# The first norm's sums and row factors: from matrix-engine transposes to x with tokens on partitions and 32x32 squares on VectorE

## The chip, the cores and the metric

The kernel runs on one core of one Trainium2 chip. The metric is the device time of one execution in microseconds (us), the median of several runs; less is better. The core has a matrix engine (PE, whose weight loads the profile lists apart as PEld), VectorE (DVE), ScalarE (ACT), GpSimd (POOL) and a queue engine (SP) that issues most of the transfers.

## What is computed

One layer of a hybrid encoder on 512 tokens of width 1024, in float32. What matters here is its beginning:

```python
def rms_norm(x, g):
    y = xf * lax.rsqrt(jnp.mean(xf * xf, axis=-1, keepdims=True) + EPS)
    return (y * g.astype(jnp.float32)).astype(x.dtype)
...
h = rms_norm(x, attn_norm_g[l])
proj = h @ w_in[l]
xr, gate, q, k, v = jnp.split(proj, [...], axis=-1)
xr = centred_depthwise_conv(xr, conv_w[l], conv_b[l])
h_f = rg_lru(xr, ...)
```

Then come the recurrent gates and scans, dilated attention, an output projection and an MLP, each with norms of its own. The factor of the first norm, one number for each token, is `rsqrt(mean(x*x) + EPS)`.

## The kernel before, in words

**Products.** The first operand of the projection is x turned, features on the 128 partitions and the 512 tokens along the row, eight tiles `k`. It is multiplied by the gain `g` but not by the token's factor; that factor is applied to the results. Each float32 operand is split into a high and a low part and each product is three matmuls (`mm3`: high by high, high by low, low by high; lines L312, L313, L314). A chunk of weights is 128x1024 numbers (512 KB) in a tile `wraw`; its high part `whi` is written by `conv_hi` (on ACT, L247, or for chunks 4, 7, 8, 9 on DVE, L245) and its low part `wlo` by `conv_lo` (DVE, L269). After the low part is made, `emit_dma` issues the load of a later chunk on SP.

**The first tiles.** `cvx(k)` makes the high and low parts of x tile k and of the first three weight columns that come with it (tiles `tw` and `wraw`, loaded at L341). PE accumulates four blocks of results, `pxr[0]` to `pxr[3]`: the first three during the pass over k (L453, then `mm3`), the fourth afterwards with chunk 3 of the weights (`xmm`). After them it goes on with chunk 4 (tile `pp`, the gate's first block).

**The first norm before.** After each `cvx(k)`, `sq(k)` squares the x tile on ACT (L372) and `addsq` adds the squares on DVE (L375), until one 128x512 tile `sqx` holds sums over the eight tiles; what is left is the sum over the 128 partitions. PE turns that tile in four 128x128 transposes (`turned`, tile `pcs`, L430), set between two blocks of the last k; DVE adds up the rows (L435) and adds EPS (L414); POOL raises to the power -0.5 (L417, 128x4 numbers, `rcol`: tokens on partitions). For the results, which have tokens along the row, a tile is needed that holds the 512 factors in every partition: PE makes it with four more transposes from a broadcast of `rcol` (`prow`, L409) and ACT copies it to `rrow`, called `rstd` in the code (L423).

**What hangs on rstd.** `conv_a(t)` multiplies block t by `rstd` (DVE, L496) and starts the convolution on ACT (L498); `conv_b(t)` does the other three taps on DVE (L503 to L505). `lru_gates` then multiplies the four results `xc` by the gates' weights on PE (tile `pg`, L528), t = 0 to 3 in order, and ACT evacuates (L532). In PE's order this stands behind the eight steps of chunk 4 and ahead of chunk 5.

**What sets the order.** Each engine executes its instructions in the order in which the code is written, and waits for the others by semaphores. The order of PE, ACT, DVE and POOL is the program's; before the change that of SP's queue was a scheduler's.

Of the kernel before, what the change touches and what calls it, by code (L numbers as in the profile page):

```python
# [12 lines left out]
FT = mybir.dt.float32  # L13
# [85 lines left out]
def hybrid_kernel(ctx: ExitStack, tc, xw0, xw, xn, w_in, w_v, w_out, w_up, w_dn, gates, vecs, bias, fg, out):  # L99
# [13 lines left out]
    def g_(name, dt=FT, shape=(P, S)):  # L113
        return work.tile(list(shape), dt, name=name, tag="g", bufs=NG)
# [19 lines left out]
    make_identity(nc, ident)  # L134
    mhalf = consts.tile([P, 4], FT, name="mhalf")
    nc.gpsimd.memset(mhalf, -0.5)
# [191 lines left out]
    xwt, w3 = [], []  # L328
    for k in range(KD):
        if 4 <= k < 7:  # L330
            xwt.append(stream.tile([P, 1024], FT, name="wraw", tag="wraw", bufs=3)[:, :XW])
        else:
            xwt.append(work.tile([P, 1024], FT, name="tw", tag="tw", bufs=4)[:, :XW if k else XG + 3 * P])
        if k == 0:
            nc.sync.dma_start(xwt[0][:, :XG], xw0[:, :XG])
            nc.sync.dma_start(xwt[0][:, XG:], xw0[:, XG:])
            nc.gpsimd.tensor_copy(ag, xwt[0][:, S:XG])
            w03 = g_("w03")[:, :P]
            nc.sync.dma_start(w03, w_in[3][:, :P])
        else:  # L340
            nc.sync.dma_start(xwt[k], xw[k - 1])  # L341
        if k == 6:
            nc.sync.dma_start(vt, vecs)

    sqx = {}

    def cvx(k):
        x, w = xwt[k][:, :S], xwt[k][:, S if k else XG:]
        g = ag[:, k:k + 1] if k else xwt[0][:, S:S + 1]
        hi, lo = g_("w3h", FR), g_("w3l", FR)  # L350
        if k < 2:
            c = (2 * P, 3 * P)[k]
            act(h_hi[:, k, :c], x[:, :c], AF.Copy, scale=g)
            nc.vector.tensor_scalar(h_hi[:, k, c:], x[:, c:], g, None, op0=OP.mult)
            if k == 0:
                nc.vector.tensor_copy(hi[:, :2 * P], w[:, :2 * P])
                act(hi[:, 2 * P:3 * P], w[:, 2 * P:], AF.Copy)
            else:
                nc.vector.tensor_copy(hi[:, :3 * P], w)
        else:  # L360
            act(h_hi[:, k, :], x, AF.Copy, scale=g)
            act(hi[:, :3 * P], w, AF.Copy)
        stt(h_lo[:, k, :], x, g, f(h_hi)[:, k, :], op0=OP.mult, op1=OP.subtract)
        nc.vector.tensor_tensor(lo[:, :3 * P], w, f(hi)[:, :3 * P], op=OP.subtract)
        if k == 0:
            act(hi[:, 3 * P:], w03, AF.Copy)
            nc.vector.tensor_tensor(lo[:, 3 * P:], w03, f(hi)[:, 3 * P:], op=OP.subtract)
        w3.append((hi, lo))

    def sq(k):  # L370
        sqx[k] = g_("sqx")
        act(sqx[k], xwt[k][:, :S], AF.Square)  # L372

    def addsq(k):
        nc.vector.tensor_tensor(sqx[0], sqx[0], sqx.pop(k), op=OP.add)  # L375

    cvx(0)
    sq(0)
    for k in range(1, KD):
        cvx(k)  # L380
        if 5 <= k < 7:
            next(spc)
        sq(k)
        if k >= 2:
            addsq(k - 1)
    emit_dma()
    for t in range(4):
        gate_load(t)
    emit_dma()
    addsq(7)  # L390
    emit_dma()

# [12 lines left out]

    def rows_of(cols, tag):
        pr = ps_("prow", tag)
        for tt in range(4):
            nc.tensor.transpose(pr[:, tt * P:(tt + 1) * P], cols(tt), ident)  # L409
        return pr  # L410

    def rstd_cols(ssc, n):
        v = small("rv", 4)
        nc.vector.tensor_scalar(v, ssc, 1.0 / n, EPS, op0=OP.mult, op1=OP.add)  # L414
        r = consts.tile([P, 4], FT, name="rcol_%d" % st["rc"])
        st["rc"] += 1
        nc.gpsimd.tensor_tensor(r, v, mhalf, op=OP.pow)  # L417
        return r

    def row_tile(cols, tag):  # L420
        pr = rows_of(lambda tt: fan(cols, tt, 1, P), tag)
        r = g_("rrow")
        act(r, pr, AF.Copy)  # L423
        return r


    def turned(ss, tag):
        pc = ps_("pcs", tag)
        for tt in range(4):
            nc.tensor.transpose(pc[:, tt * P:(tt + 1) * P], ss[:, tt * P:(tt + 1) * P], ident)  # L430
        return pc

    def row_sums(pc):
        c = small("cs", 4)
        nc.vector.tensor_reduce(c, pc.rearrange("p (t c) -> p t c", t=4), axis=mybir.AxisListType.X, op=OP.add)  # L435
        return c

# [11 lines left out]
    for k in range(KD):  # L449
# [1386 lines left out]
```

## Time and profile before

| what | value |
|---|---|
| median of 3 runs (lowest to highest) | 523.14 us (522.76 to 523.55) |
| the profiled execution, its own time | 522.93 us |
| its span, first to last instruction | 521.1 us |
| PE busy | 514.8 us (99%) |
| DVE busy | 430.5 us (83%) |
| ACT busy | 352.3 us (68%) |
| POOL busy | 66.2 us (13%) |
| mean granted clock of PE | 0.999 |

The span is 1.8 us less than the execution's own time, and that execution lies 0.2 us below the median. Times of the trace count from the start of the span. A row of the timeline gives start, duration, engine, line, what is written and what is read, and in brackets the idle time of the engine ahead of it with what ended it. Matmuls are pipelined: the duration of one is longer than the distance from its start to the next one's, so that distance is read for what a matmul costs.

### The profile page before, as it was taken

How to read it: one execution, taken by the hardware profiler on the slowest of the kernel's cores; microseconds unless marked ns; L12 is line 12 of the kernel's file. 1: busy time of each engine (PE TensorE's matmuls, PEld its weight loads, DVE VectorE, ACT ScalarE, POOL GpSimd, SP SyncE). 2: the span in 40 equal slices, each digit the busy share in tenths (PEclk: the TensorE clock that was granted, in tenths of full speed). 3: DMA queues.
4: the chain of work that ended last, by engine and by line, in shares of the span. 5: the costliest groups of instructions: out<-in, count | busy, mean ns of one | idle time of the engine just before them, and what ended most of it. 6: DMA issues, size and time to landing. Idle time of an engine off the chain costs nothing.

```text
span 521.1 us, 8223 instructions
## 1 busy us (share of the span) xinstructions
PE 514.8 (99%) x3021; PEld 444.0 (85%) x3021; DVE 430.5 (83%) x667; ACT 352.3 (68%) x571; POOL 66.2 (13%) x89
## 2 busy tenths in 40 slices
PE   9999999999999999999999999999999999999995
PEld 7857888887778788899999888889999999888884
DVE  6998985887789998898789987789766978986885
ACT  7579946777759757685568655675667577655655
POOL 0183000000010410000300412001100300231000
PEclk9999999999999999999999999999999999999999
DMA  8736555477376799847695899967986496799704
GB/s 289 224 92 198 160 155 181 117 203 209 82 250 234 196 206 285 309 148 170 154 209 158 212 275 276 309 259 165 302 259 164 117 229 211 154 290 257 198 1 162
DMA packets 40329, 105.15 MB, mean 202 GB/s; under 512 B 5056, under 2 KB 13376, under 8 KB 40288
## 3 DMA queue, kind: packets, MB, share of 16 engines
q1 hardware_dynamic: 32448, 78.07, 44.9%
q0 software_dynamic: 7696, 26.32, 27.3%
q8 instruction: 24, 0.39, 0.3%
q10 hardware_dynamic: 144, 0.23, 0.1%
q14 instruction: 17, 0.14, 0.1%
HBM read 95.59 MB, written 4.29 MB: 192 GB/s over the span
## 4 chain that ended last, share of the span: by engine, by line
PE 99%; ACT 0%; DVE 0%; issue 0%
PE pu L312 10%; PE pu L314 10%; PE pu L313 10%; PE pd L314 10%; PE pd L312 10%; PE pd L313 10%; PE pqk L312 3%; PE pqk L314 3%; PE pqk L313 3%; PE pwo L312 3%; PE pwo L314 3%; PE pwo L313 3%; PE pav L941 2%; PE pt L841 2%; PE ps L805 2%; PE pp L312 1%
## 5 line engine op out<-in xcount | busy, mean ns | idle before, releaser
L269 DVE TENSOR_TENSOR wlo<-wraw,whi 128x1024 fp32r<-128x1024 f32 x71 | 86.5, 1219 | 22.2 <-ACT whi L247 22.0
L247 ACT ACTIVATE whi<-wraw 128x1024 fp32r<-128x1024 f32 x67 | 70.8, 1058 | 36.8 <-PE pd L314 19.0
L313 PE MATMUL pd<-wlo,ah 128*128 128x512 f32 (+1 forms) x195 | 75.2, 386 | 0.0
L312 PE MATMUL pd<-whi,ah 128*128 128x512 f32 (+1 forms) x195 | 75.2, 386 | 0.0
L314 PE MATMUL pd<-whi,al 128*128 128x512 f32 (+1 forms) x195 | 75.2, 386 | 0.0
L313 PE MATMUL pu<-hl,whi 128*128 128x256 f32 x224 | 63.4, 283 | 0.0
L314 PE MATMUL pu<-hh,wlo 128*128 128x256 f32 x224 | 63.4, 283 | 0.0
L312 PE MATMUL pu<-hh,whi 128*128 128x256 f32 x224 | 63.4, 283 | 0.0
L312 PE MATMUL pu<-h2h,whi 128*128 128x256 f32 (+1 forms) x200 | 60.1, 301 | 0.0
L313 PE MATMUL pu<-h2l,whi 128*128 128x256 f32 (+1 forms) x200 | 60.0, 300 | 0.0
L314 PE MATMUL pu<-h2h,wlo 128*128 128x256 f32 (+1 forms) x200 | 60.0, 300 | 0.0
L269 DVE TENSOR_TENSOR wlo<-tw,whi 128x1024 fp32r<-128x1024 f32 x37 | 45.2, 1222 | 17.6 <-ACT whi L247 17.6
L247 ACT ACTIVATE whi<-tw 128x1024 fp32r<-128x1024 f32 x38 | 40.1, 1058 | 24.9 <-PE pd L314 6.3
L312 PEld LDWEIGHTS pu<-hh,whi 128*128 128x128 f32 x224 | 43.0, 192 | 0.0
L313 PEld LDWEIGHTS pu<-hl,whi 128*128 128x128 f32 x224 | 43.0, 192 | 0.0
L314 PEld LDWEIGHTS pu<-hh,wlo 128*128 128x128 f32 x224 | 43.0, 192 | 0.0
L247 ACT ACTIVATE whi<-ts 128x1024 fp32r<-128x1024 f32 x24 | 25.5, 1061 | 25.9 <-PE pd L314 18.4
L313 PEld LDWEIGHTS pd<-wlo,ah 128*128 128x128 f32 x195 | 36.6, 188 | 7.4
L314 PEld LDWEIGHTS pd<-whi,al 128*128 128x128 f32 x195 | 36.6, 188 | 7.4
L312 PEld LDWEIGHTS pd<-whi,ah 128*128 128x128 f32 x195 | 36.6, 188 | 7.3
L314 PEld LDWEIGHTS pu<-h2h,wlo 128*128 128x128 f32 x200 | 38.3, 191 | 1.3
L313 PEld LDWEIGHTS pu<-h2l,whi 128*128 128x128 f32 x200 | 38.3, 191 | 1.3
(283 smaller groups left out, 1221.4 us busy)
## 6 DMA issues: line engine op xcount, KB each, us to landing
wraw<-in_w_up_dram SPq DMA_DIRECT2D x25, 512.0 KB, 4.0
ts<-in_w_dn_dram POOLq DMA_DIRECT2D x24, 512.0 KB, 12.9
wraw<-in_w_dn_dram SPq DMA_DIRECT2D x24, 512.0 KB, 10.4
tw<-in_w_up_dram SPq DMA_DIRECT2D x15, 512.0 KB, 5.3
tw<-in_w_up_dram POOLq DMA_DIRECT2D x15, 512.0 KB, 7.5
wraw<-in_w_in_dram SPq DMA_DIRECT2D x13, 512.0 KB, 3.5
ts<-in_w_dn_dram SPq DMA_DIRECT2D x8, 512.0 KB, 8.6
tw<-in_w_dn_dram SPq DMA_DIRECT2D x8, 512.0 KB, 6.8
```

What stands on the lines that cost most here:

```text
L247: act(hi, raws[i], AF.Copy)
L269: nc.vector.tensor_tensor(lo, r, f(splits[i][0]), op=OP.subtract)
L312: nc.tensor.matmul(o, lhsT=a[0], rhs=b[0], start=bool(first), stop=False, skip_group_check=on)
L313: nc.tensor.matmul(o, lhsT=a[0], rhs=b[1], start=False, stop=False, skip_group_check=on)
L314: nc.tensor.matmul(o, lhsT=a[1], rhs=b[0], start=False, stop=bool(last), skip_group_check=on)
L805: nc.tensor.matmul(pss[e][:, :NK], lhsT=qs_[p, a][r, P * qt:P * qt + P], rhs=kks[p][r, b, w:w + NK], start=i == 0, stop=i == 2)
L841: nc.tensor.transpose(pt[:, i * P:(i + 1) * P], en[h][qt][:, k:k + P], ident)
L941: nc.tensor.matmul(pav[p][a, co], lhsT=vs[:, jt, h * DH:(h + 1) * DH], rhs=et[h, jt][:, ci], start=jt == 0 and i == 0, stop=jt == 3 and i ...
```

## The change

The sums of squares are taken from a second copy of x that has tokens on partitions. `xn` is an input that the kernel had already (it is read much later for the residual); eight blocks of it, 128x512 numbers (256 KB) each, are now also loaded at the beginning as `xs`, two for each 128 tokens. A block's row sum is one instruction: on ACT a square with an accumulator for blocks 0, 1, 2, 4 and 6, on DVE a multiply with an accumulator (`tensor_tensor_reduce`) for 3, 5 and 7. They give `ss8`, 128x8 numbers. Sixteen DVE instructions of 32x4 numbers each add the two halves and EPS and copy each group of 32 partitions into all four groups (`rv16`, 128x16). POOL's power runs on those 128x16 numbers (`r16`). ACT writes each of the 16 columns 32 times (`rfan`, 128x512), and one DVE transpose of 32x32 squares makes `rstd` of it. `rcol` is copied out of `r16` by four small POOL instructions. The eight PE transposes, the ACT squares and the DVE adds of before are gone.

Other things move with it. SP's queue in this part is now in written order, with the eight loads `xs` ahead of chunk 3, and chunk 3 is loaded as two halves. Chunk 3 is converted after the sixteen small instructions: DVE makes the high and the low part of its first half and the low part of its second, ACT the high part of the second. Chunk 4 is converted after the transpose. ACT's conversion of chunk 5 comes after `conv_a(1)`.

```diff
+        def sq(i):
+            c = ss8[:, 4 * (i % 2) + i // 2:4 * (i % 2) + i // 2 + 1]
+            if i in (3, 5, 7):
+                nc.vector.tensor_tensor_reduce(xs[i], xs[i], xs[i], 1.0 / D, 0.0, OP.mult, OP.add, c)
+            else:
+                act(xs[i], xs[i], AF.Square, scale=D ** -0.5, accum_out=c)
...
-    def sq(k):
-        sqx[k] = g_("sqx")
-        act(sqx[k], xwt[k][:, :S], AF.Square)
-
-    def addsq(k):
-        nc.vector.tensor_tensor(sqx[0], sqx[0], sqx.pop(k), op=OP.add)
...
+        for i in range(8):
+            load_xs(i)
+        plain.popleft()
+        raws[3] = stream.tile([P, 1024], FT, name="wraw", tag="wraw", bufs=3)
+        for c in (slice(0, S), slice(S, 2 * S)):
+            nc.sync.dma_start(raws[3][:, c], w_in[3][:, c])
...
-            if k == KD - 1 and t == 0:
-                sqt = turned(sqx[0], "et")
...
-    conv_hi(3)
-    conv_lo(3)
-    rcol = rstd_cols(row_sums(sqt), D)
+    for i in range(8):
+        sq(i)
+    rv16 = small("rv16", 16)
+    for a in range(4):
+        r = slice(32 * a, 32 * a + 32)
+        for b in range(4):
+            stt(by_group(rv16)[32 * b:32 * b + 32, a], ss8[r, :4], EPS, ss8[r, 4:], op0=OP.add, op1=OP.add)
+    r16 = consts.tile([P, 16], FT, name="r16")
+    nc.gpsimd.tensor_tensor(r16, rv16, mhalf, op=OP.pow)
+    hi, lo = [stream.tile([P, 1024], FR, name=n, tag=n, bufs=4) for n in ("whi", "wlo")]
+    r = raws.pop(3)
+    splits[3] = (hi, lo)
+    c = slice(0, S)
+    nc.vector.tensor_copy(hi[:, c], r[:, c])
+    nc.vector.tensor_tensor(lo[:, c], r[:, c], f(hi)[:, c], op=OP.subtract)
+    c = slice(S, 2 * S)
+    act(hi[:, c], r[:, c], AF.Copy)
+    nc.vector.tensor_tensor(lo[:, c], r[:, c], f(hi)[:, c], op=OP.subtract)
+    emit_dma()
+    rfan, rstd = g_("rfan"), g_("rrow")
+    act(rfan.rearrange("p (b i) -> p b i", i=32), fan(r16, 0, 16, 32), AF.Copy)
+    nc.vector.transpose(rstd, rfan)
     conv_hi(4)
-    conv_hi(5)
     nc.gpsimd.dma_start(bt, bias)
     conv_lo(4)
-    xmm(range(1, 3))
-    rstd = row_tile(rcol, "et")
+    xmm(range(1, 2))
     conv_a(0, pxr[0])
     conv_a(1, pxr[1])
+    conv_hi(5)
     next(spc)
     cneg, chalf = next(spc)
+    rcol = consts.tile([P, 4], FT, name="rcol")
+    for a in range(4):
+        r = slice(32 * a, 32 * a + 32)
+        nc.gpsimd.tensor_copy(rcol[r], by_group(r16)[r, a])
     conv_b(0)
     act(warm, epsb, AF.Sigmoid)
-    xmm(range(3, KD))
+    xmm(range(2, KD))
```

On PE, at the last k of the first pass and at the beginning of chunk 3, the difference reads as follows (`whi` and `wlo` are the parts of chunk 3 here):

```order
 L313 MATMUL pxr<-h_lo,w3h 128x512
 L314 MATMUL pxr<-h_hi,w3l 128x512
-L430 MATMUL pcs<-ident,sqx 128x128 x4
 L312 MATMUL pxr<-h_hi,w3h 128x512
 L313 MATMUL pxr<-h_lo,w3h 128x512
```

The four transposes go; the second four, L409, go in the same way from between the second and the third step of chunk 3, and nothing else moves on PE.

On DVE, from the end of `cvx(7)` to the first use of `rstd`, the order before was this (`sqx` the squares, `wraw` to `wlo` at L269 first chunk 3 and then chunk 4):

```order
L364 TENSOR_TENSOR w3l<-tw,w3h 128x384
L375 TENSOR_TENSOR sqx<-sqx 128x512 x2
L269 TENSOR_TENSOR wlo<-wraw,whi 128x1024
L435 TENSOR_REDUCE cs<-pcs 128x4
L414 TENSOR_SCALAR rv<-cs 128x4
L245 CAST whi<-wraw 128x1024
L269 TENSOR_TENSOR wlo<-wraw,whi 128x1024
L496 TENSOR_TENSOR xr<-pxr,rrow 128x2x256 x2
```

And it is now this (`ss_127` is `ss8`, `rv_306` is `rv16`; the rows L665 to L669 are chunk 3, L245 and L269 chunk 4):

```order
L358 ISA xs,ss_127<-xs 128x512
L358 ISA ss_127 128x1
L658 SCALAR_TENSOR_TENSOR rv_306<-ss_127 32x4 x16
L665 CAST whi<-wraw 128x512
L666 TENSOR_TENSOR wlo<-wraw,whi 128x512
L669 TENSOR_TENSOR wlo<-wraw,whi 128x512
L673 STREAM_TRANSPOSE rrow<-rfan 128x512
L245 CAST whi<-wraw 128x1024
L269 TENSOR_TENSOR wlo<-wraw,whi 128x1024
L482 TENSOR_TENSOR xr<-pxr,rrow 128x2x256 x2
```

All of chunk 3's work on DVE moved behind the sums and the sixteen small instructions, and all of chunk 4's behind the transpose.

On SP the loads ahead of the gates' weights were these (`tw` at L341 is the last x tile):

```order
L341 DMA wraw<-in_xw_dram 128x896 x3
L343 DMA vt<-in_vecs_dram 128x60
L341 DMA tw<-in_xw_dram 128x896
L230 DMA wraw<-in_w_in_dram 128x1024 x3
L320 DMA gwr<-in_gates_dram 128x256 x4
```

They are now these:

```order
L342 DMA wraw<-in_xw_dram 128x896 x3
L347 DMA vt<-in_vecs_dram 128x60
L342 DMA tw<-in_xw_dram 128x896
L353 DMA xs<-in_xn_dram 128x512 x8
L396 DMA wraw<-in_w_in_dram 128x512 x2
L230 DMA wraw<-in_w_in_dram 128x1024
L320 DMA gwr<-in_gates_dram 128x256 x4
```

Eight loads of 256 KB stand ahead of chunk 3, and chunk 5 moved behind the gates' weights.

More of the change, by code (lines that the diff above doesn't have):

```diff
@@ L328, in hybrid_kernel, with load_xw @@
     xwt, w3 = [], []
-    for k in range(KD):
+    w03 = g_("w03")[:, :P]
+    def load_xw(k):
         if 4 <= k < 7:
@@ L416, in rstd_cols, with by_group @@
         st["rc"] += 1
-        nc.gpsimd.tensor_tensor(r, v, mhalf, op=OP.pow)
+        nc.gpsimd.tensor_tensor(r, v, mhalf[:, :4], op=OP.pow)
         return r
[L420 to L436, printed above, removed]
+    def by_group(t):
+        return t.rearrange("p (t a) -> p a t", a=4)
     def col_sums(ss):
```

86 lines of the change are left out of this document (40 added, 46 removed).

## The prediction

> **What bounds the kernel now.** I read the page first: its busy shares and the chain that ended last.
>
> ```profile
> span 521.1 us, 8223 instructions
> PE 514.8 (99%) x3021; PEld 444.0 (85%) x3021; DVE 430.5 (83%) x667; ACT 352.3 (68%) x571; POOL 66.2 (13%) x89
> PE 99%; ACT 0%; DVE 0%; issue 0%
> ```
>
> PE is the bound from one end to the other. Work taken off ACT, DVE or POOL is therefore worth nothing by itself. A change counts by what it takes out of PE's stream and by the waits that it puts in there. Next I read the timeline of PE at the two places where the transposes stand.
>
> ```profile
> 20.34 0.39 PE L314 MATMUL pxr<-h_hi,w3l 128*128 128x512 f32 x1
> 20.57 0.60 PE L430 MATMUL pcs<-ident,sqx 128*128 128x128 f32 x4
> 20.93 0.48 PE L312 MATMUL pxr<-h_hi,w3h 128*128 128x512 f32 x1
> ...
> 23.56 0.39 PE L314 MATMUL pxr<-h_hi,wlo 128*128 128x512 f32 x1
> 23.78 0.60 PE L409 MATMUL prow<-ident,rcol 128*128 128x128 f32 x4
> 24.14 0.47 PE L312 MATMUL pxr<-h_hi,whi 128*128 128x512 f32 x1
> ```
>
> By their starts, four transposes take 20.93 - 20.57 = 0.36 us and the other four 24.14 - 23.78 = 0.36 us, with PE waiting for nothing at either place. The third thing that I read is when PE asks for the results that the change moves: chunk 3, chunk 4, and the gates' inputs. These are rows of PE's weight loads.
>
> ```profile
> 22.17 0.19 PEld L312 LDWEIGHTS pxr<-h_hi,whi 128*128 128x128 f32 x1
> 27.44 0.19 PEld L312 LDWEIGHTS pp<-h_hi,whi 128*128 128x128 f32 x1
> 37.97 0.15 PEld L528 LDWEIGHTS pg<-xc,gwr 64*64 64x64 f32 x4 [0.28 <-ACT ga L532]
> 40.22 0.19 PEld L312 LDWEIGHTS pp<-h_hi,whi 128*128 128x128 f32 x1 [0.81 <-ACT ga L532]
> ```
>
> At 22.17 it wants chunk 3, at 27.44 chunk 4. Of the gates' 64 recorded passes, sixteen for each block t, the last sixteen (t = 3) begin at 37.97. At 40.22 it goes on with chunk 5.
>
> **Term 1, the transposes.** Eight go: 2 x 0.36 = 0.72 us off PE. The skill puts another price on them: the Trainium skill (TensorE: Matmul & The Clock Gate, Part 4: PE-mode transpose) gives about 275 ns for one in a kernel, 2.2 us for eight, and the sum would gain 1.5 us more by it. The starts above decide against that: between other matmuls one takes 0.09 us.
>
> The squares on ACT and adds on DVE that go were beside PE's work, so I count them at nothing. They make both engines free sooner, and then the loads decide.
>
> **Term 2, when the sums are there.** Eight loads of 256 KB come behind the x tiles in one queue. The windows of the DMA, the issue of the last x tile and its time to landing:
>
> ```profile
> 7.00:12.00 5.00, 5.00 (x23) 3.81 (x23) 4.76 (x9) 4.87 (x10) 0.00 (x0) 1.00 1.03 409
> 12.00:14.00 2.00, 2.00 (x11) 1.65 (x10) 2.00 (x5) 2.00 (x5) 0.00 (x0) 1.00 0.28 107
> 6.22 0.33 SPq L341 DMA_DIRECT2D tw<-in_xw_dram  x1
> tw<-in_xw_dram SPq DMA_DIRECT2D x1, 448.0 KB, 7.4
> ```
>
> With transfers queued the DMA engines are full (1.03) at 409 GB/s. At 12.0 there are 2 x 107 = 214 KB of x tiles left, so at that rate they end at 12.5. The last one's landing is known at 6.22 + 7.4 = 13.6, 1.1 later. The eight new blocks are 8 x 262 = 2,097 KB, 5.1 us at 409 GB/s: the last ends at 17.65 and has landed at about 18.75. Before that, DVE and ACT have finished the x tiles, whose last lands at 13.6, and are working off the earlier blocks as they land.
>
> ```profile
> L821 DVE CUSTOM_DVE_ANT_0 e<-ps,tw 128x416 f32<-128x416 f32 x32 | 16.7, 587 | 0.2
> L821 DVE DVE_READ_ACCUMULATOR2_ANT mn<- 128x1 f32 x32 | 2.7, 83 | 0.0
> L1290 ACT ACTIVATE scr<-x1n 128x512 f32<-128x512 f32 x8 | 5.0, 629 | 0.0
> L1290 ACT ACTIVATION_READ_ACCUMULATOR scr<-x1n 128x1 f32 x8 | 1.6, 199 | 0.0
> ```
>
> The kernel has both instructions already. On DVE block 7 takes 0.587 x 512/416 + 0.083 = 0.80 us: 19.55. On ACT five take at most 5 x 0.83 = 4.1 us; beginning at 13.6 + 1.2 for the last x tile that gives 18.9, and block 6, the last of them, lands one block (0.64 us) ahead of block 7. So DVE's block 7 is last, 19.55.
>
> **Term 3, the sixteen small instructions.** They stand ahead of chunk 3 on DVE. The trace has two prices for a small one:
>
> ```profile
> 145.18 0.73 DVE L445 TENSOR_TENSOR cs<-cu 32x4 f32<-32x4 f32 x4
> 145.94 0.17 DVE L414 TENSOR_SCALAR rv<-cs 128x4 f32<-128x4 f32 x1
> ...
> 15.05 0.16 DVE L150 SCALAR_TENSOR_TENSOR e<-vt 128x8 f32<-128x8 f32 x1
> 15.13 0.16 DVE L151 TENSOR_SCALAR sp<-vt 128x8 f32<-128x8 f32 x1
> ```
>
> Four adds of 32x4, each into another group of 32 partitions, take 145.94 - 145.18 = 0.76 us, 0.19 each. Two small ones over all partitions begin 0.08 apart. The new ones are 32x4 and change the group with each instruction, so I take 0.19: 16 x 0.19 = 3.0 us, and 22.6; the other end is 16 x 0.08 = 1.3 us, and 20.85. The Trainium skill (VectorE: DVE Perf Modes, Two Vector instructions with no wait between them) has a rule that speaks against the change: an instruction whose output starts in another group of 32 partitions than the one before it starts only when all earlier ones have finished. By that rule all sixteen pay the row's 0.19, and without it the term would be 1.7 us smaller; the L445 rows agree with it.
>
> **Term 4, PE at chunk 3.** Rows for the conversion:
>
> ```profile
> L245 DVE CAST whi<-wraw 128x1024 fp32r<-128x1024 f32 x4 | 2.7, 684 | 0.0
> L359 DVE CAST w3h<-tw 128x384 fp32r<-128x384 f32 x1 | 0.4, 351 | 0.0
> L375 DVE TENSOR_TENSOR sqx<-sqx 128x512 f32<-128x512 f32 x7 | 4.8, 684 | 0.1
> L269 DVE TENSOR_TENSOR wlo<-wraw,whi 128x1024 fp32r<-128x1024 f32 x71 | 86.5, 1219 | 22.2 <-ACT whi L247 22.0
> ```
>
> The first half's high part (128x512) lies between the casts, about 0.42 us: 23.05. PE, without the first four transposes, asks at 22.17 - 0.36 = 21.81 and waits 1.24 us. The low part takes 0.68 us: 23.7. PE asks for it two matmuls later, two times the distance 20.57 - 20.34 = 0.23, at 23.5, and waits another 0.2. In all 1.44 us; the second half is ready long before PE is there. With the 0.72 gained, PE comes to chunk 4 at 27.44 + 0.72 = 28.16.
>
> **Term 5, rstd and what hangs on it.** POOL's power is the least known price. Its rows (the second is a plain multiply of 128x8), then the copy, a transpose and the places on DVE:
>
> ```profile
> L417 POOL TENSOR_TENSOR rcol<-rv,mhalf x2: 1343/1644/1945, 22.3 to 146.2; 128x4 f32<-128x4 f32 x2
> L163 POOL TENSOR_TENSOR pl<-pl,z x8: 203/538/676, 29.1 to 36.8; 128x8 f32<-128x8 f32 x8
> L372 ACT ACTIVATE sqx<-tw 128x512 f32<-128x512 f32 x5 | 3.1, 617 | 0.0
> L440 DVE STREAM_TRANSPOSE cst<-ysq 128x512 f32<-128x512 f32 x2 | 1.4, 690 | 0.0
> 25.05 1.29 DVE L496 TENSOR_TENSOR xr<-pxr,rrow 128x512 f32<-128x512 f32 x2 [1.09 <-ACT rrow L423]
> 36.70 0.75 DVE L505 SCALAR_TENSOR_TENSOR xc<-xr,vt,xc 128x511 f32<-128x511 f32 x1
> ```
>
> If its time is all fixed, 128x16 costs 1.34 us; if all but the 0.20 of the shortest multiply grows with the columns, 0.20 + 4 x 1.14 = 4.8. I take 2.2, nearer to the two rows of the operation itself (1.34 and 1.95) than to the stretched value. From 22.6: power to 24.8, ACT's copy (0.62) to 25.4, DVE's transpose (0.69) to 26.1, chunk 4's high part (0.68) to 26.8 and low part (1.22) to 28.0. PE wants the former at 28.16 and the latter two matmuls after that, so chunk 4 does not stall. But `conv_a(0)` now starts at 28.0 and not at 25.05, 2.95 us later, and from there DVE is busy without a pause to the end of `conv_b(3)` at 36.70 + 0.75 = 37.45. That becomes 40.4. PE, 0.72 late, wants it for the gates' last block at 37.97 + 0.72 = 38.7: a wait of 1.7, and PE is 2.4 late there. What is not clear is the idle 0.81 behind the gates: if ACT's pace sets it, it takes up that much of the wait (PE 1.6 late), if PE's own change between the two kinds of matmul does, nothing. I take the middle, 2.0.
>
> **Sum.** Off 0.72, on 1.44 at chunk 3 and 1.3 at the gates: +2.0 us. Beyond the gates I count nothing: SP loads chunk 3's successor later, but ACT needs that one (31.0 before) only after `conv_a(3)`, which is later too. The moved loads of chunk 5 and the gates' weights are 2 MB, 5 us, later at most, and are wanted at 40 and 33. The profiled execution's 522.93 becomes 524.9. It lies 0.2 below the median of the runs, and a forecast for the median is 525.1.
>
> A measurement of this kernel can tell about 0.2% (1.05 us) from no change.
>
> **Rivals.**
>
> *The waits are covered.* The small instructions run at 0.08, so DVE has the high part of chunk 3 at 21.25, and PE does not wait there. With a power of 1.34 to 2.2 us, `conv_a(0)` is 0.3 to 1.2 late and `conv_b(3)` ends at 37.75 to 38.65, against PE's 37.25 (0.72 early): PE ends between 0.7 early and 0.7 late, the time at 522.4 to 523.8. For it speaks that DVE has 5 us less to do before; against it speak the L445 rows, and that the last block cannot land before the bytes ahead of it are through. Chance 0.27.
>
> *The power takes long.* At 4.8 us, the transpose ends at 28.7, chunk 4's parts at 29.4 and 30.6. PE at chunk 4 waits 1.2 + 0.75, is 2.7 late, and `conv_b(3)` ends at 43.0: PE is 4.2 to 5.0 late, the time at 527.3 to 528.1. This mechanism decides from about 2.3 us of power on, where chunk 4 begins to stall. For it: the multiply of 128x8 can take 0.20, so most of the 1.34 is the power itself. Chance 0.13.
>
> *Faster by over 0.2%.* Each transpose holds PE for the whole of its recorded duration:
>
> ```profile
> L430 PE MATMUL pcs<-ident,sqx x4: 270/272/273, 20.6 to 20.9; 128*128 128x128 f32 x4
> ```
>
> Eight times 0.272 is 2.18 us, and if the waits are covered as above the time is 521.0. This is what the skill's figure of Term 1 comes to. The starts, 0.09 apart, speak against it, and it needs the cover besides. It would also be faster if the waits are covered and a start of PE that hung on ACT or DVE were to go. Chance 0.08.
>
> **Numbers.** My forecast, +0.77 (a power of 1.34, all of the 0.81 absorbed) to +3.4 (a power of 3 us), has 0.52 with 525.1 as the likeliest; 523.9 to 526.5 is its own range. The whole range goes from 522.4, the lower end of the covered case, to 527.3, the lower end of the long power; what lies outside is the faster case and most of the long power, under 0.2. Faster: 0.08. Same: the covered case, 0.27. Slower: 0.52 + 0.13 = 0.65; the edge of my own case that falls under 1.05 is small and I leave it there.
>
> **What would show it.** In the changed trace: no L409 or L430; the last `xs` landing near 18.8; sixteen L658 over about 3 us; PE's load for chunk 3 idle over 1 us ahead of it, ended by DVE's cast L665; `conv_a(0)` near 28; the gates' last block waiting for DVE's L491. I am wrong if PE's load for chunk 3 shows no idle time, if the sixteen take under 2 us, or if the last block of `xs` lands before 17.6.

## The result, and the profile after

The changed kernel takes 526.75 us (median of 6 runs, 526.27 to 527.04), the kernel before 523.05 (6 runs, 522.75 to 523.55). The ratio is 1.0069, 95% interval 1.0058 to 1.0080: slower by 3.7 us. The profiled execution took 526.27 us with a span of 524.5 (before: 522.93 and 521.1), so the traces differ by 3.4 us. The profiled execution is the fastest of the six; the other 0.3 us of the 3.7 stand in no trace.

From the page of the changed kernel, the chain that ended last, by engines:

```profile
PE 92%; DMA 2%; DVE 1%; ACT 1%; SPq 1%; POOL 1%; issue 0%; DVEq 0%; POOLq 0%
```

PE was 99% of that chain before and stood nearly alone in it. Now 8% of it belongs to the others. In order of time the chain begins with SP's queue and the transfers of the last x tile and of the last `xs`, and goes on with the sum, the power, the copy, the transpose and `conv_a(0)`; PE comes behind these. That is the changed part.

The timeline of DVE in the changed kernel, from the last block of `xs` to `conv_a(0)`, and the end of `conv_b(3)`:

```profile
18.75 0.69 DVE L358 CUSTOM_DVE_ANT_0 xs<-xs 128x512 f32<-128x512 f32 x1 [0.65 <-DMA xs<-in_xn_dram]
...
19.56 2.72 DVE L658 SCALAR_TENSOR_TENSOR rv<-ss 32x4 f32<-32x4 f32 x16
...
26.23 0.71 DVE L673 STREAM_TRANSPOSE rrow<-rfan 128x512 f32<-128x512 f32 x1 [2.17 <-ACT rfan L672]
26.87 0.65 DVE L245 CAST whi<-wraw 128x1024 fp32r<-128x1024 f32 x1
27.55 1.23 DVE L269 TENSOR_TENSOR wlo<-wraw,whi 128x1024 fp32r<-128x1024 f32 x1
28.69 1.28 DVE L482 TENSOR_TENSOR xr<-pxr,rrow 128x512 f32<-128x512 f32 x2
...
40.33 0.75 DVE L491 SCALAR_TENSOR_TENSOR xc<-xr,vt,xc 128x511 f32<-128x511 f32 x1
```

The last block is summed as soon as it has landed; the sixteen small instructions take 2.72 us; then DVE stands still for 2.17 us, while POOL and ACT work. These are their rows:

```profile
22.44 3.10 POOL L660 TENSOR_TENSOR r<-rv,mhalf 128x16 f32<-128x16 f32 x1 [18.71 <-DVE rv L658]
```

```profile
25.57 0.63 ACT L672 ACTIVATE rfan<-r 128x512 f32<-128x512 f32 x1 [4.84 <-POOL r L660]
```

The power takes 3.10 us, and `conv_a(0)` (the first of the two at L482) starts at 28.69, 3.64 us later than before (25.05).

Now PE's weight loads in the changed kernel at the places where it waits:

```profile
22.79 0.19 PEld L312 LDWEIGHTS pxr<-h_hi,whi 128*128 128x128 f32 x1 [1.47 <-DVE whi L665]
23.52 0.19 PEld L314 LDWEIGHTS pxr<-h_hi,wlo 128*128 128x128 f32 x1 [0.43 <-DVE wlo L666]
29.43 0.19 PEld L312 LDWEIGHTS pp<-h_hi,whi 128*128 128x128 f32 x1 [1.73 <-DVE xr L482]
...
41.15 0.24 PEld L514 LDWEIGHTS pg<-xc,gwr 64*64 64x64 f32 x8 [1.56 <-ACT ga L518]
...
43.06 0.19 PEld L312 LDWEIGHTS pp<-h_hi,whi 128*128 128x128 f32 x1 [0.81 <-ACT ga L518]
```

The first two waits, at chunk 3, and the one at 41.15, right behind the end of `conv_b(3)` (40.33 + 0.75 = 41.08), were foreseen. The releaser that the row at 41.15 names, an ACT evacuation, I take for the other semaphore only; the one that ends last is DVE's L491. The runs below bear that out: in the changed kernel and in all nine experiments that have this wait, it ends 0.07 to 0.08 us behind the end of `conv_b(3)`, while from PE's first gate pass, after which ACT's evacuations begin, it is about 6.0 us in most, but 5.2 in e5_late_chunk3 and 7.1 in e4_other_slot. The wait at 29.43 was not foreseen. It is the first matmul of chunk 4, and it waits neither for the high nor for the low part of chunk 4, but for `conv_a(0)`: `pp` takes the PSUM slot of `pxr[0]`, and `conv_a(0)` must have read that first. Chunk 5 begins at 43.06, against 40.22 before: 2.84 later. From there on the distances are those of before to 0.1 us: the last outputs are issued 2.95 later. The remaining 0.45 of the 3.4 lie behind that issue (first row before, second row changed):

```profile
517.18 0.81 SPq L1512 DMA_DIRECT2D out_dram<-tw  x2
```

```profile
520.13 0.81 SPq L1520 DMA_DIRECT2D out_dram<-tw  x2
```

Before, the span ends 3.92 us behind it, in the changed kernel 4.37. In both the transfers are through about 2.4 us behind it (the DMA engines' share is 0.01 or less from 519.6 on before and 0.00 from 522.6 on after), so the output itself is not slower: the difference lies in the stretch after the last transfer.

### The profile page after: what moved, and what is told of

Read it like the earlier page. It is cut to its first block, busy times and chain, and to the rows that moved or that the text cites. A ratio compares the mean times of both kernels' runs of the same rounds, so it can differ in the third digit from the quotient of the medians.

```text
span 524.5 us, 8233 instructions
## 1 busy us (share of the span) xinstructions
PE 514.4 (98%) x3013; PEld 442.6 (84%) x3013; DVE 431.1 (82%) x683; ACT 351.3 (67%) x573; POOL 70.8 (13%) x93
## 4 chain that ended last, share of the span: by engine, by line
PE 92%; DMA 2%; DVE 1%; ACT 1%; SPq 1%; POOL 1%; issue 0%; DVEq 0%; POOLq 0%
PE pu L313 10%; PE pu L312 10%; PE pu L314 10%; PE pd L312 10%; PE pd L313 10%; PE pd L314 10%; PE pqk L312 3%; PE pqk L314 3%; PE pqk L313 3%; PE pwo L312 3%; PE pwo L314 3%; PE pwo L313 3%; PE pav L949 2%; PE pt L849 2%; PE ps L813 2%; PE pp L312 1%
## 5 line engine op out<-in xcount | busy, mean ns | idle before, releaser
L269 DVE TENSOR_TENSOR wlo<-wraw,whi 128x1024 fp32r<-128x1024 f32 x70 | 85.2, 1219 | 23.1 <-ACT whi L247 22.9
L247 ACT ACTIVATE whi<-wraw 128x1024 fp32r<-128x1024 f32 x66 | 69.7, 1058 | 34.0 <-PE pd L314 18.2
L269 DVE TENSOR_TENSOR wlo<-tw,whi 128x1024 fp32r<-128x1024 f32 x37 | 45.2, 1222 | 17.2 <-ACT whi L247 17.2
L312 PEld LDWEIGHTS pu<-h2h,whi 128*128 128x128 f32 x200 | 38.3, 191 | 1.3
```

The source lines that it names most:

```text
L247: act(hi, raws[i], AF.Copy)
L269: nc.vector.tensor_tensor(lo, r, f(splits[i][0]), op=OP.subtract)
L312: nc.tensor.matmul(o, lhsT=a[0], rhs=b[0], start=bool(first), stop=False, skip_group_check=on)
```

## The experiments

**The theory** after the two traces: the whole loss comes by one path, the late `conv_a(0)`. From there DVE works without a pause to the end of `conv_b(3)`, PE waits for that, does the gates' last block and goes on with chunk 5, 43.06 - 28.69 = 14.37 us behind the start of `conv_a(0)`. Before, it was 40.22 - 25.05 = 15.17, so that path had 0.80 us to spare: 3.64 - 0.80 = 2.84. PE's waits at chunk 3 and chunk 4 lie ahead in the same stretch and cost nothing of their own, since what they don't take, the gates' wait takes. **The rivals**: those two waits count by themselves; the transposes were dear or cheap in another way than I had it; the new order of the loads has a share. Each ratio below is to executions of the kernel before that were taken beside the run; the differences in us to the changed kernel are between medians that were not.

### What the transposes cost: e1_twice_turned

The kernel before with each of its eight transposes executed twice. Apart from that, a price was to be had here: powers on POOL in three sizes, at a place where nothing waits for POOL.

```diff
     def rows_of(cols, tag):
...
-        for tt in range(4):
+        for tt in (0, 1, 2, 3, 0, 1, 2, 3):
             nc.tensor.transpose(pr[:, tt * P:(tt + 1) * P], cols(tt), ident)
...
     def turned(ss, tag):
...
-        for tt in range(4):
+        for tt in (0, 1, 2, 3, 0, 1, 2, 3):
             nc.tensor.transpose(pc[:, tt * P:(tt + 1) * P], ss[:, tt * P:(tt + 1) * P], ident)
...
+        for n in (4, 16, 32, 4, 16, 32):
+            nc.gpsimd.tensor_tensor(po[:, :n], two[:, :n], mh[:, :n], op=OP.pow)
```

> The kernel before with every one of its eight PE transposes done twice into the same place, and, far from them (after the bias rows are stored, when GpSimd has nothing to do for a long time), six powers on GpSimd of 128x4, 128x16 and 128x32 numbers, twice. Theory (a transpose costs the distance between starts): 8 x 0.09 = 0.72 us longer than before, span about 521.8, and each group of eight takes 0.72 between its neighbours. Rival (it costs its recorded duration, 0.27): 2.2 us longer, span about 523.3. The powers: if the time grows with the columns above a fixed part, as 1.3 to 1.9 for 4 and 3.1 for 16 columns suggest, 128x32 takes about 5 us; if the 3.1 was mostly waiting for DVE, 16 and 32 columns lie close together.

Measured: 524.07 us, ratio 1.0015 (1.0006 to 1.0024) to the kernel before, 0.7 us longer. The timeline of PE in this run:

```profile
20.29 1.03 PE L430 MATMUL pcs<-ident,sqx 128*128 128x128 f32 x8
21.07 0.48 PE L312 MATMUL pxr<-h_hi,w3h 128*128 128x512 f32 x1
```

Eight take 21.07 - 20.29 = 0.78 us by their starts, where four took 0.36. Eight transposes are worth about 0.7 us, as the theory had it, and not 2.2. POOL's powers in this run, by their line:

```profile
L474 POOL TENSOR_TENSOR po<-two,mh x6: 1107/3454/6198, 48.3 to 64.2; 128x4 f32<-128x4 f32 x2, 128x16 f32<-128x16 f32 x2, 128x32 f32<-128x32 f32 x2
```

They start at 48.32, 50.27, 54.25, 59.95, 61.14 and 64.22, in the order of the code and with less than 0.1 us between two. So the two on 128x4 took 1.9 and 1.1 us, the two on 128x16 3.9 and 3.0, the two on 128x32 5.6 and 6.2: the same power can differ by most of a microsecond. By the means (1.5, 3.45, 5.9) most of the time grows with the columns, about 0.16 us a column, and an estimated 0.9 us is fixed.

### What makes a small instruction dear: e2_same_group and e2b_no_rewrite

Two tries at the sixteen small instructions, which now run over all partitions and change no group. In the first, the four copies of a group go to one and the same place.

```diff
-            stt(by_group(rv16)[32 * b:32 * b + 32, a], ss8[r, :4], EPS, ss8[r, 4:], op0=OP.add, op1=OP.add)
+            stt(by_group(rv16)[:, a], ss8[:, :4], EPS, ss8[:, 4:], op0=OP.add, op1=OP.add)
```

> The changed kernel with the sixteen small instructions kept in number but each over all 128 partitions, 128x4, so that none changes the group of 32 partitions. It leaves out the copying between groups, so the factors go to the wrong tokens. Theory (the change of group costs the overlap of one instruction with the next): the sixteen take 1.3 us and not 2.7, chunk 3's cast and conv_a(0) come 1.4 us earlier, the wait at chunk 3 all but goes, and the span is 1.4 us shorter than the changed kernel's, about 523.1. Rival (a small instruction costs 0.17 whatever it writes): no change, 524.5.

Measured: 527.04 us, ratio 1.0072 (1.0058 to 1.0086). DVE's row, from its timeline:

```profile
20.27 2.79 DVE L658 SCALAR_TENSOR_TENSOR rv<-ss 128x4 f32<-128x4 f32 x16
```

Nothing was gained, and taken alone that would speak against the change of group. But the edit had put something else in its place: four instructions in a row write the same numbers. The starts show what that costs: the twelve that follow one with the same place begin 0.19 to 0.21 us behind it, the three that go on to a new place 0.08. So the run does not tell the theories apart, and the next has a place for each.

```diff
-    for a in range(4):
-        r = slice(32 * a, 32 * a + 32)
-        for b in range(4):
-            stt(by_group(rv16)[32 * b:32 * b + 32, a], ss8[r, :4], EPS, ss8[r, 4:], op0=OP.add, op1=OP.add)
+    rest = consts.tile([P, 64], FT, name="rest")
+    for n in range(16):
+        o = by_group(rv16)[:, n // 4] if n % 4 == 0 else rest[:, 4 * n:4 * n + 4]
+        stt(o, ss8[:, :4], EPS, ss8[:, 4:], op0=OP.add, op1=OP.add)
```

> The changed kernel with its sixteen small instructions each over all 128 partitions and each into a place of its own: no change of the group of 32 partitions and no repeated write. It leaves out the copying between the groups, so that the factors go to wrong tokens; the number of instructions and all work behind them are the same. Theory (the change of group sets their pitch): the sixteen take 16 x 0.08 = 1.3 us in place of 2.72, conv_a(0) begins 1.4 us earlier than in the changed kernel (about 27.3 when the last block of xs lands at 18.75), PE goes on with chunk 5 14.4 us behind it, and the time is 1.4 us shorter, a ratio of about 1.004 to the kernel before. Rival (a small instruction takes 0.17 whatever its partitions): nothing changes, ratio 1.007.

Measured: 525.42 us, ratio 1.0042 (1.0026 to 1.0057). The first and the last of the sixteen and what follows, from DVE's timeline:

```profile
20.13 0.17 DVE L658 SCALAR_TENSOR_TENSOR rv<-ss 128x4 f32<-128x4 f32 x1
20.21 0.30 DVE L658 SCALAR_TENSOR_TENSOR rest<-ss 128x4 f32<-128x4 f32 x3
...
21.08 0.31 DVE L658 SCALAR_TENSOR_TENSOR rest<-ss 128x4 f32<-128x4 f32 x3
21.30 0.43 DVE L665 CAST whi<-wraw 128x512 fp32r<-128x512 f32 x1
...
27.68 1.28 DVE L482 TENSOR_TENSOR xr<-pxr,rrow 128x512 f32<-128x512 f32 x2
```

The sixteen now take 21.30 - 20.13 = 1.17 us, 0.07 each, where they took 0.17 in the changed kernel. From the first of them to `conv_a(0)` it is 7.55 us in place of 9.13, and the time falls by 1.3. So in the changed kernel each begins about when the one ahead is through (0.16 us by its duration), and here well before that. The edit takes away the change of group and makes 128x4 of 32x4; that the smaller shape alone would cost the 0.10 is not excluded by a run, since no run has 32x4 instructions that stay in one group. The change of group is the rule of the Trainium skill that the prediction used (VectorE: DVE Perf Modes, Two Vector instructions with no wait between them); the changed kernel and this one agree with it, at 0.17 and 0.07.

### Where PE's wait at chunk 4 goes: e4_other_slot

The changed kernel with the first block of the gate in another PSUM slot, one that is free early; the slots of the other gate results are dealt out anew to fit.

```diff
-    PG = ("gs", "et", "gs", "et", "pj", "pj", "pj", "gs", "et", "gs", "et", "pj", "pj", "pj", "pj", "gs")
+    PG = ("gs", "et", "gs", "pj", "pj", "pj", "pj", "gs", "gs", "pj", "pj", "et", "pj", "pj", "et", "gs")
...
-    gsteps = [th for t in range(4) for th in proj_thunks(C_G + t, "et" if t == 1 else "pj", gate_done(t), t > 1)]
+    gsteps = [th for t in range(4) for th in proj_thunks(C_G + t, ("et", "gs", "pj", "pj")[t], gate_done(t), t > 1)]
```

> The changed kernel with chunk 4's results in a PSUM slot that is free, not in the one that conv_a(0) has to read first; the gates' slots are dealt out anew to fit. Theory (all three waits of PE lie one behind the other on one path, DVE's convolution chain, and only the last of them counts): PE's wait at chunk 4 falls from 1.6 to about 0.4 us (then for DVE's low part of chunk 4), the wait at the gates' last block grows by as much, and the time stays as in the changed kernel within 0.2 us, span 524.5. Rival (each wait counts by itself): 1.2 us shorter, 523.3.

Measured: 527.17 us, ratio 1.0072 (1.0058 to 1.0086). PE's weight loads that wait:

```profile
29.44 0.19 PEld L314 LDWEIGHTS pp<-h_hi,wlo 128*128 128x128 f32 x1 [0.68 <-DVE wlo L269]
36.85 0.24 PEld L514 LDWEIGHTS pg<-xc,gwr 64*64 64x64 f32 x8 [1.13 <-ACT whi L247]
...
41.75 0.24 PEld L514 LDWEIGHTS pg<-xc,gwr 64*64 64x64 f32 x8 [1.74 <-ACT ga L518]
43.66 0.19 PEld L312 LDWEIGHTS pp<-h_hi,whi 128*128 128x128 f32 x1 [0.81 <-ACT ga L518]
```

The wait for the slot is gone: chunk 4 waits 0.68 us for its own low part. What PE gained there it stands still later, at the gates' blocks. `conv_a(0)` began at 29.30 in this execution, and chunk 5 came 14.36 us after it. The slot was a real wait, without a price.

### Whether the wait at chunk 3 has a price: e5_late_chunk3

The changed kernel with two more adds of 128x512 on DVE ahead of chunk 3's conversion, 1.42 us that DVE takes out of its idle time before the transpose.

```diff
+    for _ in range(2):
+        nc.vector.tensor_tensor(xs[7], xs[3], xs[5], op=OP.add)
     nc.vector.tensor_copy(hi[:, c], r[:, c])
```

> The changed kernel with two more DVE adds of 128x512 (1.3 us, their result is not used) ahead of the cast of chunk 3. DVE has 2.2 us of idle time ahead of the transpose, so what follows from there does not move. Theory (only the path through conv_a and conv_b counts): PE waits 1.3 us longer at chunk 3 and 1.3 us less at chunk 4, and the time stays within 0.2 us, span 524.5. Rival (the wait at chunk 3 counts by itself): 1.3 us longer, 525.8.

Measured: 526.76 us, ratio 1.0064 (1.0048 to 1.0080), as the changed kernel. PE's weight loads:

```profile
24.37 0.19 PEld L312 LDWEIGHTS pxr<-h_hi,whi 128*128 128x128 f32 x1 [2.73 <-DVE whi L667]
...
41.66 0.24 PEld L514 LDWEIGHTS pg<-xc,gwr 64*64 64x64 f32 x8 [0.74 <-ACT ga L518]
43.57 0.19 PEld L312 LDWEIGHTS pp<-h_hi,whi 128*128 128x128 f32 x1 [0.81 <-ACT ga L518]
```

The wait at chunk 3 grew by 1.26 us; the one at chunk 4 is gone, and the one at the gates' last block fell from 1.56 to 0.74. The time stayed. `conv_a(0)` stands at 29.21, 0.52 later than in the changed kernel, and not by the two adds: the last `xs` landed at 18.99 (0.24 later) and the power took 3.36 (0.26 longer), while DVE still stood idle for 1.10 ahead of the transpose. Chunk 5 came 14.36 us behind `conv_a(0)` once more.

### Chunk 4 into the idle time: e3_chunk4_first

The changed kernel, with chunk 4's conversion ahead of the transpose.

```diff
+    nc.gpsimd.dma_start(bt, bias)
+    conv_hi(4)
+    conv_lo(4)
     nc.vector.transpose(rstd, rfan)
-    conv_hi(4)
-    nc.gpsimd.dma_start(bt, bias)
-    conv_lo(4)
```

> The changed kernel with chunk 4's conversion (high and low part, 1.9 us on DVE) written ahead of the transpose, into the 2.2 us in which DVE waits for POOL and ACT. Theory (DVE's chain from conv_a(0) on sets when PE goes on with chunk 5): with the sums at the same time conv_a(0) begins right after the transpose, at about 26.9 in place of 28.7; PE's gates and chunk 5 come 1.6 to 1.8 us earlier, chunk 5 begins 14.4 us after conv_a(0), and the time is 1.6 to 1.8 us shorter: about 525.0, ratio 1.0035. Rival (the waits of PE at chunk 3, 1.9 us, and at chunk 4 set the loss by themselves): chunk 3's wait stays and the time is within 0.4 us of the changed kernel's.

Measured: 525.07 us, ratio 1.0039 (1.0025 to 1.0053), 1.7 us shorter than the changed kernel. DVE in this run:

```profile
24.33 0.69 DVE L245 CAST whi<-wraw 128x1024 fp32r<-128x1024 f32 x1
25.05 1.23 DVE L269 TENSOR_TENSOR wlo<-wraw,whi 128x1024 fp32r<-128x1024 f32 x1
26.58 0.71 DVE L676 STREAM_TRANSPOSE rrow<-rfan 128x512 f32<-128x512 f32 x1 [0.30 <-ACT rfan L672]
27.39 1.29 DVE L482 TENSOR_TENSOR xr<-pxr,rrow 128x512 f32<-128x512 f32 x2
```

DVE's idle time of 2.17 us is down to 0.30. The first small instruction stood at 19.90 here, so `conv_a(0)` begins 27.39 - 19.90 = 7.49 us after it (9.13 in the changed kernel), though PE waits for chunk 3 as before:

```profile
23.14 0.19 PEld L312 LDWEIGHTS pxr<-h_hi,whi 128*128 128x128 f32 x1 [1.57 <-DVE whi L665]
```

That is against the rival, by which the time would have stayed.

### The power first: e6_power_first

The add and the power on 128x4 numbers at once, chunk 3's conversion beside the power, and the sixteen copies of the finished factors after that.

```diff
-    rv16 = small("rv16", 16)
-    for a in range(4):
-        r = slice(32 * a, 32 * a + 32)
-        for b in range(4):
-            stt(by_group(rv16)[32 * b:32 * b + 32, a], ss8[r, :4], EPS, ss8[r, 4:], op0=OP.add, op1=OP.add)
+    v4 = small("rv", 4)
+    stt(v4, ss8[:, :4], EPS, ss8[:, 4:], op0=OP.add, op1=OP.add)
     r16 = consts.tile([P, 16], FT, name="r16")
-    nc.gpsimd.tensor_tensor(r16, rv16, mhalf, op=OP.pow)
+    rcol = consts.tile([P, 4], FT, name="rcol")
+    nc.gpsimd.tensor_tensor(rcol, v4, mhalf[:, :4], op=OP.pow)
...
     emit_dma()
+    for a in range(4):
+        r = slice(32 * a, 32 * a + 32)
+        for b in range(4):
+            nc.vector.tensor_copy(by_group(r16)[32 * b:32 * b + 32, a], rcol[r])
...
-    rcol = consts.tile([P, 4], FT, name="rcol")
-    for a in range(4):
-        r = slice(32 * a, 32 * a + 32)
-        nc.gpsimd.tensor_copy(rcol[r], by_group(r16)[r, a])
```

> The changed kernel with the power on 128x4 numbers right after one add on DVE, chunk 3 converted while POOL works, and then the sixteen copies between the groups, as plain copies of the finished factors. POOL's four small copies are gone. Theory (DVE's chain): the wait of PE at chunk 3 goes (about 0.2 left of 1.5), the power takes 1.1 to 1.9 us, chunk 3's three instructions 1.8 us beside it, the sixteen copies 2.7, ACT's copy 0.6, the transpose 0.7, chunk 4's parts 1.9: conv_a(0) begins about 1.2 us earlier than in the changed kernel, and the time is 1.2 us shorter, about 525.5, ratio 1.0045. Rival (chunk 3's wait counts by itself besides): 1.2 + 1.4 = 2.6 us shorter, ratio 1.002.

Measured: 526.02 us, ratio 1.0051 (1.0037 to 1.0064), 0.7 us shorter than the changed kernel. DVE in this run:

```profile
20.73 0.16 DVE L655 SCALAR_TENSOR_TENSOR rv<-ss 128x4 f32<-128x4 f32 x1
...
22.55 2.94 DVE L672 COPY r<-rcol 32x4 f32<-32x4 f32 x16
26.18 0.71 DVE L675 STREAM_TRANSPOSE rrow<-rfan 128x512 f32<-128x512 f32 x1 [0.70 <-ACT rfan L674]
...
28.65 1.28 DVE L482 TENSOR_TENSOR xr<-pxr,rrow 128x512 f32<-128x512 f32 x2
```

From the first small instruction to `conv_a(0)` it is 7.92 us, 1.21 less, as expected. But this execution had its last block of `xs` at 19.92, 1.17 later than the profiled execution of the changed kernel, so that its trace shows nearly the same `conv_a(0)`. PE's load for chunk 3 has no wait at all:

```profile
22.51 0.19 PEld L312 LDWEIGHTS pxr<-h_hi,whi 128*128 128x128 f32 x1
```

The time fell by 0.7 us where the theory had 1.2, though the theory's ratio, 1.0045, lies inside the interval and the rival's, 1.002, does not: to be rid of that wait is worth nothing that shows by itself.

### All of it: e8_all and e9_conv_ahead

The kernel before this with six of the sixteen copies on ACT and chunk 4's high part ahead of the transpose:

```diff
+            if b < 2 or (a, b) in ((0, 2), (1, 2)):
+                nc.vector.tensor_copy(o, rcol[r])
+            else:
+                act(o, rcol[r], AF.Copy)
...
-    nc.vector.transpose(rstd, rfan)
-    conv_hi(4)
     nc.gpsimd.dma_start(bt, bias)
+    conv_hi(4)
+    nc.vector.transpose(rstd, rfan)
     conv_lo(4)
```

> The kernel with the power first, as in the run before it, with six of the sixteen copies on ACT and chunk 4's high part ahead of the transpose. Theory: DVE's part between the sums and conv_a(0) is then 0.2 + 1.8 + 1.7 + 0.7 + 0.7 + 1.2 = 6.3 us where it is 9.1 in the changed kernel: conv_a(0) at about 25.9, chunk 5 at 40.2, where the kernel before has it: the time within 0.5 us of the kernel before, ratio 0.999 to 1.001. Rival (something else of the change than the late conv_a(0) costs, such as the loads' new order): it stays over 1 us slower than before.

Measured: 524.12 us, ratio 1.0018 (1.0009 to 1.0027). DVE's rows and PE's return to chunk 5:

```profile
19.73 0.16 DVE L655 SCALAR_TENSOR_TENSOR rv<-ss 128x4 f32<-128x4 f32 x1
...
25.92 1.28 DVE L482 TENSOR_TENSOR xr<-pxr,rrow 128x512 f32<-128x512 f32 x2
```

```profile
40.29 0.19 PEld L312 LDWEIGHTS pp<-h_hi,whi 128*128 128x128 f32 x1 [0.81 <-ACT ga L518]
```

From the first small instruction to `conv_a(0)` it is 6.19 us, and chunk 5 begins where it did before. 2.6 of the 3.7 us have come back. The time is still 0.95 us over that of before, nearly twice the 0.5 that I expected and just under the rival's 1, so this run alone does not rule out that something else of the change costs up to a microsecond. The profiled execution, the fastest of the eleven (span 521.7, 0.6 over before), has chunk 5 0.07 late, the issue of the last outputs 0.2, and 0.4 behind that issue, as in the changed kernel. The other 0.35 of the medians stand in no trace.

The last version lets ACT make chunk 4's high part, puts `conv_a(0)` ahead of chunk 4's low part and one of chunk 3's three instructions behind the copies:

```diff
     act(hi[:, c], r[:, c], AF.Copy)
-    nc.vector.tensor_tensor(lo[:, c], r[:, c], f(hi)[:, c], op=OP.subtract)
     emit_dma()
...
+    nc.vector.tensor_tensor(lo[:, c], r[:, c], f(hi)[:, c], op=OP.subtract)
...
-    conv_hi(4)
+    hi4 = stream.tile([P, 1024], FR, name="whi", tag="whi", bufs=4)
+    act(hi4, raws[4], AF.Copy)
+    splits[4] = (hi4,)
     nc.vector.transpose(rstd, rfan)
-    conv_lo(4)
     xmm(range(1, 2))
     conv_a(0, pxr[0])
+    conv_lo(4)
     conv_a(1, pxr[1])
```

> As the kernel with the power first, six copies on ACT and chunk 4's high part early, and three moves more: that high part is made by ACT, the second half of chunk 3's low part stands behind the copies, and conv_a(0) stands ahead of chunk 4's low part. Theory: DVE has 0.7 us less to do up to conv_b(3), of which 0.3 is lost in waiting for the transpose's input: chunk 5 begins 0.35 us earlier than there with the sums at the same time, ratio to before about 1.001. PE cannot gain more than its eight transposes, 0.72 us, on the kernel before. Rival (PE's wait for chunk 4's low part takes the place of the wait for the slot and is as long): no change.

Measured: 523.51 us, ratio 1.0004 (0.9996 to 1.0013): no difference from the kernel before that can be told. Its first small instruction and PE's return to chunk 5:

```profile
19.98 0.16 DVE L655 SCALAR_TENSOR_TENSOR rv<-ss 128x4 f32<-128x4 f32 x1
```

```profile
40.12 0.19 PEld L312 LDWEIGHTS pp<-h_hi,whi 128*128 128x128 f32 x1 [0.81 <-ACT ga L518]
```

DVE's chain is 0.42 us shorter (chunk 5 comes 20.14 us after the first small instruction, 20.56 in the version ahead of it). PE's rows show no wait at chunk 4 here, so the rival's wait for the low part did not arise. No version here beats the kernel before. What could still be won is small: PE with no wait at all would reach chunk 5 at 40.22 - 0.72 = 39.5, and 0.4 us are lost again at the end.

### The late convolution alone: e10_late_conv

The other direction: the kernel before, with its transposes, squares and loads, and seven adds on DVE that make `conv_a(0)` as late as in the changed kernel.

```diff
     conv_lo(4)
+    for _ in range(7):
+        nc.vector.tensor_tensor(sqx[0], f(splits[4][0])[:, :S], f(splits[4][0])[:, S:], op=OP.add)
     xmm(range(1, 3))
```

> The kernel before with one thing of the change alone, the late conv_a(0): seven extra adds of 128x512 on DVE (0.71 us each, 5.0 in all) behind chunk 4's low part and ahead of conv_a(0). The transposes, the loads and all else are as before. Theory (the late conv_a(0) is the whole of PE's delay): conv_a(0) begins at 24.0 + 5.0 = 28.9, chunk 5 14.4 us behind it, at 43.3, 3.1 later than before; the time is 3.1 us longer, ratio 1.0059. Rival (the new order of the loads, or chunk 3's late parts, have a share): it stays under 2 us.

Measured: 525.97 us, ratio 1.0057 (1.0038 to 1.0077). DVE's and PE's rows:

```profile
24.11 5.05 DVE L674 TENSOR_TENSOR sqx<-whi 128x512 f32<-128x512 f32 x7
29.07 1.28 DVE L496 TENSOR_TENSOR xr<-pxr,rrow 128x512 f32<-128x512 f32 x2
```

```profile
43.43 0.19 PEld L312 LDWEIGHTS pp<-h_hi,whi 128*128 128x128 f32 x1 [0.81 <-ACT ga L532]
```

The last is PE's return to chunk 5, 14.36 us behind `conv_a(0)` and 3.21 later than before. The late convolution alone costs 3.2 us in the trace, as the theory said; by the medians it is 2.6, and the interval of the ratio means 2.0 to 4.0 us. So up to chunk 5 the loads' order and chunk 3 need no share of their own. For the whole time these runs can't say that to better than about a microsecond.

The same distance in the profiled executions (times in us; the last column is the span less the start of `conv_a(0)`):

| kernel | `conv_a(0)` | chunk 5 | distance | span | span less `conv_a(0)` |
|---|---|---|---|---|---|
| before | 25.05 | 40.22 | 15.17 | 521.1 | 496.05 |
| after | 28.69 | 43.06 | 14.37 | 524.5 | 495.81 |
| e1_twice_turned | 25.60 | 40.75 | 15.15 | 521.8 | 496.20 |
| e2_same_group | 29.35 | 43.71 | 14.36 | 525.2 | 495.85 |
| e2b_no_rewrite | 27.68 | 42.06 | 14.38 | 523.5 | 495.82 |
| e3_chunk4_first | 27.39 | 41.77 | 14.38 | 523.2 | 495.81 |
| e4_other_slot | 29.30 | 43.66 | 14.36 | 525.1 | 495.80 |
| e5_late_chunk3 | 29.21 | 43.57 | 14.36 | 525.0 | 495.79 |
| e6_power_first | 28.65 | 43.01 | 14.36 | 524.5 | 495.85 |
| e8_all | 25.92 | 40.29 | 14.37 | 521.7 | 495.78 |
| e10_late_conv | 29.07 | 43.43 | 14.36 | 524.3 | 495.23 |

Before and in e1_twice_turned PE sets the pace there and the chain has time to spare. In e9_conv_ahead a low part of 1.2 us stands between `conv_a(0)` and `conv_a(1)`, so it has another distance. The kernels with the eight new loads end 0.6 later behind `conv_a(0)` than e10_late_conv, which has not got them. That 0.6 is what the late convolution does not explain; 0.4 of it is the part behind the last issue of outputs.

## Why the prediction was right, and where it fell short

The direction and the path were right; the loss was put at 2.0 us and is 3.4 in the trace, 3.7 in the medians. The measured 526.75 lies above the range of the forecast's own case (523.9 to 526.5) and inside the whole one only (up to 527.3). The steps that failed are sizes: the power, what hides behind the gates, and the end of the program, which was counted at nothing.

- **The transposes (Term 1)**: right. 0.72 us by their starts, about 0.7 by doubling them (e1_twice_turned). In the changed kernel the gain is not seen in the time, since PE waits it away at the gates. The 275 ns apiece that the Trainium skill gives (TensorE: Matmul & The Clock Gate, Part 4: PE-mode transpose) agrees with the recorded duration of one here, 0.272 us, but is not its price between other matmuls.
- **The sums (Term 2)**: right, the last block landed by 18.75, as worked out from the bytes. That it fits to the hundredth is luck: in the nine profiled executions with these loads the block landed between 18.75 and 19.92, with 19.16 in the middle, and the chain moves with it, since it hangs on that block.
- **The sixteen small ones (Term 3)**: 2.72 us where I had 3.0. e2b_no_rewrite supports the cause, the change of group; the share of the smaller shape was not taken apart.
- **Chunk 3 (Term 4)**: the wait is there as worked out (it ends at 22.79, I had 23.05; 1.47 + 0.43 us, I had 1.44). That PE would ask for chunk 4 next and not stall there failed: PE waits 1.73 us for a PSUM slot that `conv_a(0)` must free. I had looked only at the operands of a matmul, not at who still reads the place it writes. By e4_other_slot the miss has no price that shows, because the gates' wait takes up what that one leaves.
- **The power (Term 5)**: mis-sized. I took 2.2 us between 1.34 and 4.8; it is 3.10. With the small instructions 0.28 shorter this put `conv_a(0)` at 28.69 and not at 28.0.
- **What hides behind the gates (Term 5)**: I let half of the idle 0.81 behind the gates absorb a part of the wait. It absorbs nothing: the row has 0.81 before, after and in all ten kernels of the experiments, however long the wait ahead of it. What it consists of is not shown. In its place the path had 0.80 to spare where I had counted 37.97 - 37.45 = 0.52. The rows say why: from the first load of the gates' last block to chunk 5 it is 40.22 - 37.97 = 2.25 before and 43.06 - 41.15 = 1.91 behind the wait, so PE makes up 0.34 there, less the 0.07 from DVE's end to PE's load.
- **The sum**: my terms at chunk 5 were 2.95 of lateness less 0.52, 2.43, and the half absorbed made 2.0. Measured are 3.64 less 0.80, 2.84: the later `conv_a(0)` adds 0.69, the absorbing 0.41, and the larger slack takes 0.28 off. Behind chunk 5 another 0.1 and, at the end, 0.45 come on top, for which I had counted nothing. By the same terms the upper end, a power of 3 us and nothing absorbed, comes to 3.75 - 0.52 = 3.2 and not 3.4.
- **The rivals**: "covered" and "faster" fell with the small instructions at 0.17 and the transposes at 0.09; "the power takes long" is half of what happened: 3.10 is over the point that I gave for it, but chunk 4's stall, which I priced there, had none. The point was wrong too: by the terms of the prediction chunk 4's low part, ready at 28.0 and wanted at 28.6, stalls PE from a power of about 2.8 us on, not 2.3.

The 0.45 us behind the last issue of outputs stay open. They show in every profiled kernel with the eight `xs` loads (4.3 to 4.4 us from that issue to the end) and neither before (3.92) nor in e1_twice_turned nor e10_late_conv (3.94). Between the end of the last transfer and the end of the span no row and no transfer stands in the trace, and no run here takes that stretch apart.

## What to carry to other kernels

Where the bound engine waits several times in a row for the same late chain, only the last wait counts: find the instruction from which the distance to the end is constant (here `conv_a(0)`), and price a change by what it does to that instruction's start. Look then for what stands ahead of it in the same queue without need: moving chunk 4's conversion into idle time gave back 1.7 of 3.7 us, with not an instruction less. And run an operation that is priced by the column before its operand is copied out, not after.

## What the runs showed of the hardware

- POOL's power costs mostly by its columns: 1.1 to 1.9 us for 128x4, 3.0 to 3.9 for 128x16, 5.6 to 6.2 for 128x32 (e1_twice_turned; 3.10 for 128x16 in the changed kernel).
- A small DVE instruction of 128x4 numbers starts 0.07 us behind the one ahead (e2b_no_rewrite), and 0.20 behind it when both write the same place (e2_same_group). One of 32x4 numbers whose output changes the group of 32 partitions starts 0.17 behind (the changed kernel).
- The same load, with the same bytes ahead of it in its queue, landed up to 1.2 us apart in nine profiled executions, at nearly the same granted clock of PE (0.995 to 0.999). The chain that hangs on it moves along: `conv_a(0)` comes 9.94 us behind the landing in the changed kernel and in e4_other_slot, which landed 0.61 later. That whole runs spread more by it is not shown: the eleven of e8_all lie 2.1 us apart and the kernel before beside them 1.2, but the eleven of e9_conv_ahead 1.2 and the kernel before beside them 1.6.
